# A hybrid decoder layer on one core: 80 small weight columns stored as 128, and another order of steps

## The chip, the cores and the metric

The kernel runs on one core of one Trainium2 chip. The time is the device time of one execution in microseconds. A run is one execution; the kernel before has three of them, and one more execution was taken with the profiler on. TensorE (PE in the views) multiplies, VectorE (DVE), ScalarE (ACT) and GpSimd (POOL) do the rest, and SyncE (SP) issues the transfers. Each engine works through its own queue in order.

## What is computed

One layer: an adaptive RMSNorm of x, one projection into all the small parts, two head groups side by side, and an output projection with a gated, normalised residual. Group A is a gated delta rule with chunks; group B picks 256 keys for each query with an indexer and attends to latents.

```python
mod = silu(c) @ w_ada + b_ada
shift, scale, gate = split(mod, 3)
h = rmsnorm(x, g_pre) * (1 + scale) + shift
qkv_a, z_a, b_a, a_a, q_b, ckv, z_b, iq, ik, iw = split(h @ w_in)
o_a = gated_deltanet(qkv_a, z_a, b_a, a_a, ...)     # conv, l2norm, triangular inverse per chunk, recurrence
o_b = dsa_sparse_attention(q_b, ckv, iq, ik, iw, ...)  # indexer score, top 256, softmax, w_uv
x = x + gate * rmsnorm(concat(o_a, o_b) @ w_out, g_post)
```

There are 1024 tokens and 1024 model columns; group A has 4 heads of 128 with chunks of 64, group B 4 heads of 128 and 8 indexer heads of 64. All is float32; large products are split into a high and a low part and done as three matmuls.

## The kernel before

The work is cut into named steps, and the table `PLAN` (lines 37 to 42) gives the order in which they are written down. A step is the next piece of a Python generator: `D0` and `D1` are the two token halves of the indexer keys, `F` the first token half of four convolutions, `X` the second token half of h, `I` the indexer scores (12 pieces), `S` the bitwise search for the 256th score (20), `K`, `J`, `Q`, `V`, `M`, `R`, `N`, `A` with a 0 or 1 the keys, the inverse, the queries, the values, the merge of the inverse's blocks, the recurrence, the norm and the mixing of a pair of group A's heads, `Z` its gates, `HZ` and `HQ` the gates and queries of group B, `C` the latents, `G` the residual gate, `T` an attention block and `O` an output block. A scheduler then interleaves what the steps issue within each engine's queue. A second table, `ENGINES`, names for 281 places (a split, an add, a copy) the engine that does it, where it is not the usual one.

Weights come as 25 tiles of 128 columns, fetched in the order in which the steps of `PLAN` need them, one raw tile ahead and two split ones. `split` (236 to 239, by the helpers at 174 to 181) makes a high part by a cast and a low part by a difference. `proj` (lines 421 to 433) does a half of 512 tokens: for each of the eight chunks of 128 model columns one matmul of the high weights with the high part of h (line 430), one with its low part (431), one of the low weights (432), into one of two PSUM banks. Whoever reads the bank last sets it free for the half after the next one.

The places that matter here:

- `wsp` (lines 391 to 398) holds 80 columns: 64 of the indexer key, 8 of its weights, 8 of group A's decay and write gates. `key_half` (440 to 450) runs `proj` on it, 24 matmuls for each token half, and copies the parts out. The host puts the 80 columns together in `laid_out`.
- `first_halves` (749 to 768) runs one-column products (line 754) for the first halves of four convolutions.
- `second_half` (452 to 466) transposes x on TensorE (line 311), makes h's high part on ACT (459), a float32 copy on VectorE (460) and the low part on POOL or VectorE (site `xl`).
- `conv_half` (704 to 731) scales the projection's bank and adds three shifted copies, on VectorE (line 189) or on ACT and POOL (192, 193).
- `invert` (858 to 878) is a chain of 60 POOL instructions, then two transfers through DRAM; `merge` (914 to 946) begins with a VectorE transpose of what came back (919) and goes on with small matmuls (926 to 942) and VectorE copies (927, 939). `recur` (948 to 1000) is a chain of 128-column matmuls, VectorE and ACT.
- `search` counts on VectorE (607) and ACT (619), and ends with six blocks of a comparison, a scan and two more passes (691 to 696).

## Time and profile before

| | us |
|---|---|
| median of 3 runs | 738.63 |
| the runs | 738.37, 738.63, 744.95 |
| the profiled execution | 746.19 |
| its span, first to last instruction | 744.5 |
| TensorE busy in it | 685.7 |
| VectorE busy | 529.7 |
| ACT busy | 436.9 |
| POOL busy | 336.3 |

The profiled execution is 7.6 us above the median, and 1.7 us of it lie outside the span. The granted clock is a share of 2.4 GHz; 0.50 is 1.2 GHz, the lower of the two levels that the rows show. A matmul's duration contains a part that overlaps the next one: in a dense row 512 columns start 0.23 us apart at the full clock and 0.43 at half.

### The profile page before, as it was taken

The page shows a single profiled execution, that of the slowest core. Times are in us where ns is not written, and L with a number is a line of the kernel's source. Part 1 is how long each engine was busy: PE and PEld are TensorE (multiplying, and loading weights), DVE is VectorE, ACT ScalarE, POOL GpSimd, SP SyncE. Part 2 cuts the span into 40 slices and gives each one's busy share as a digit, 9 for nine tenths or more (in the row PEclk, how much of TensorE's full clock was granted, in tenths as well). Part 3 has the DMA queues.
Part 4 walks back from the last instruction along what each step waited for, and adds up shares of the span by engine and source line. Part 5 has one row for each costly group of instructions (what it writes and reads, how often), then busy time and mean ns, then how long its engine had stood idle before and what let it go on. Part 6 is the DMA issues. An engine that isn't in the chain of part 4 may idle for free.

```text
span 744.5 us, 11292 instructions
## 1 busy us (share of the span) xinstructions
PE 685.7 (92%) x3863; PEld 574.7 (77%) x3863; DVE 529.7 (71%) x1342; ACT 436.9 (59%) x863; POOL 336.3 (45%) x395
## 2 busy tenths in 40 slices
PE   3999898999999899998998999988887999999996
PEld 2887787888778678876787878777765889888885
DVE  3977785663356866868689887877889999964212
ACT  4545584576668888859868494523336687434211
POOL 2146616456997300314432599941243232654310
PEclk9996999999999999999999999996799999999999
DMA  8931000013112111220032212276033205313311
GB/s 309 405 153 44 1 29 28 1 40 104 42 47 96 43 68 47 90 81 29 1 114 113 86 57 86 71 250 235 15 115 114 85 29 185 114 61 124 141 58 56
DMA packets 35287, 70.10 MB, mean 94 GB/s; under 512 B 11431, under 2 KB 18717, under 8 KB 35230
## 3 DMA queue, kind: packets, MB, share of 16 engines
q1 hardware_dynamic: 35230, 69.39, 26.5%
q8 instruction: 30, 0.49, 0.3%
q14 instruction: 27, 0.22, 0.1%
HBM read 53.64 MB, written 15.73 MB: 93 GB/s over the span
## 4 chain that ended last, share of the span: by engine, by line
PE 54%; DVE 16%; POOL 11%; DMA 6%; ACT 6%; issue 5%; SPq 1%; DVEq 0%; POOLq 0%; ACTq 0%
PE ps L430 8%; PE ps L432 8%; PE ps L431 8%; PE ps L1281 4%; PE ps L1279 4%; PE ps L1280 4%; POOL ns L869 4%; POOL rk L867 4%; ACT junk L619 2%; DVE pr L1217 1%; PE ps L1234 1%; DMA wraw<-in_w_tiles_dram 1%; DMA wa<-in_w_ada_dram 1%; DVE junk L607 1%; PE ps L579 1%
## 5 line engine op out<-in xcount | busy, mean ns | idle before, releaser
L430 PE MATMUL ps<-h,whi 128*128 128x512 f32 (+2 forms) x448 | 177.2, 396 | 12.8 <-DVE cv L189 6.7
L431 PE MATMUL ps<-h,whi 128*128 128x512 f32 (+2 forms) x448 | 177.0, 395 | 0.0
L432 PE MATMUL ps<-h,wlo 128*128 128x512 f32 (+2 forms) x448 | 176.0, 393 | 0.7 <-POOL wlo L181 0.7
L619 ACT ACTIVATE junk<-score,pat,sgn 128x1024 bf16<-128x1024 f32 (+2 forms) x93 | 105.5, 1135 | 11.5 <-DVE pat L660 10.3
L430 PEld LDWEIGHTS ps<-h,whi 128*128 128x128 f32 (+1 forms) x448 | 85.5, 191 | 34.2 <-DVE cv L189 7.8
L432 PEld LDWEIGHTS ps<-h,wlo 128*128 128x128 f32 (+1 forms) x448 | 85.4, 191 | 17.3 <-issue 0.9
L431 PEld LDWEIGHTS ps<-h,whi 128*128 128x128 f32 (+1 forms) x448 | 85.4, 191 | 15.9 <-issue 0.7
L607 DVE TENSOR_SCALAR_CACHE_REDUCE junk<-score,pat 128x640 bf16<-128x640 f32 (+2 forms) x93 | 68.8, 740 | 1.6
L193 POOL TENSOR_TENSOR cv<-cv,tmp 128x510 f32<-128x510 f32 (+2 forms) x33 | 39.1, 1186 | 42.6 <-ACT tmp L192 42.3
L1281 PE MATMUL ps<-woh,ml 128*128 128x512 f32 x128 | 49.9, 392 | 1.3 <-DVE ml L181 1.3
L590 ACT ACTIVATE ps<-ps 128x512 f32<-128x512 f32 (+3 forms) x70 | 34.1, 511 | 28.5 <-PE ps L580 27.9
L1280 PE MATMUL ps<-wol,mh 128*128 128x512 f32 x128 | 50.4, 394 | 0.0
L1279 PE MATMUL ps<-woh,mh 128*128 128x512 f32 x128 | 50.0, 393 | 0.0
L193 POOL TENSOR_TENSOR score<-score,tmp 128x512 f32<-128x512 f32 (+3 forms) x29 | 32.4, 1123 | 35.0 <-ACT tmp L192 30.7
L189 DVE SCALAR_TENSOR_TENSOR score<-ps,iw,score 128x384 f32<-128x384 f32 (+3 forms) x41 | 25.7, 643 | 28.1 <-ACT ps L590 22.8
L869 POOL TENSOR_TENSOR ns<-ns,rk 64x30 f32<-64x30 f32 (+14 forms) x60 | 36.1, 602 | 3.8
L181 POOL TENSOR_TENSOR wlo<-wraw,whi 128x1024 fp32r<-128x1024 f32 (+1 forms) x11 | 25.7, 2340 | 26.7 <-PE ps L432 19.9
L867 POOL TENSOR_TENSOR rk<-ns 64x30 f32<-64x30 f32 (+14 forms) x60 | 36.2, 604 | 3.2
L189 DVE SCALAR_TENSOR_TENSOR cv<-ps,cols,cv 128x511 f32<-128x511 f32 (+2 forms) x39 | 28.8, 738 | 6.2 <-POOL cv L193 4.3
L174 ACT ACTIVATE whi<-wraw 128x1024 fp32r<-128x1024 f32 x19 | 20.0, 1054 | 20.1 <-PE ps L431 12.7
L1283 ACT ACTIVATE junk<-ps 128x512 bf16<-128x512 f32 x16 | 9.5, 595 | 36.8 <-PE ps L1281 32.3
L181 DVE TENSOR_TENSOR wlo<-wraw,whi 128x1024 fp32r<-128x1024 f32 x19 | 24.7, 1299 | 8.7 <-ACT whi L174 7.8
(358 smaller groups left out, 1742.1 us busy)
## 6 DMA issues: line engine op xcount, KB each, us to landing
wraw<-in_w_tiles_dram SPq DMA_DIRECT2D x29, 512.0 KB, 3.5
wa<-in_ada_tiles_dram SPq DMA_DIRECT2D x16, 512.0 KB, 10.2
x<-in_x_dram SPq DMA_DIRECT2D x8, 512.0 KB, 3.3
qd<-qo SPq DMA_DIRECT2D x8, 512.0 KB, 3.0
wa<-in_w_ada_dram SPq DMA_DIRECT2D x8, 512.0 KB, 5.1
qb<-qd SPq DMA_DIRECT2D x8, 512.0 KB, 3.2
woraw<-in_w_out_dram SPq DMA_DIRECT2D x8, 512.0 KB, 3.4
xr<-in_x_dram SPq DMA_DIRECT2D x8, 512.0 KB, 3.9
```

The source lines that it names most:

```text
L189: V.scalar_tensor_tensor(o, a, scale, o, op0=ALU.mult, op1=ALU.add)
L193: G.tensor_tensor(o, o, tmp, op=ALU.add)
L430: mm(o, lhsT=hi[:, k, :], rhs=h[:, 0, c0:c1], start=(k == 0), stop=False)
L431: mm(o, lhsT=hi[:, k, :], rhs=h[:, 1, c0:c1], start=False, stop=False)
L432: mm(o, lhsT=lo[:, k, :], rhs=h[:, 0, c0:c1], start=False, stop=(k == NK - 1))
L607: V.tensor_scalar(junk[:, 0:src.shape[1]], src, t, None, op0=op, op1=ALU.add, accum_out=o)
L619: A.activation(junk[:, 0:(b + 1) * P], score[b], AF.Sign, scale=sg, bias=t, accum_out=o)
L867: G.tensor_tensor(tmp, ns[:, 0:i, i:i + 1].to_broadcast([64, i, w]), ns[:, i:i + 1, i + 1:32].to_broadcast([64, i, w]), op=ALU.mult)
L869: G.tensor_tensor(ns[:, 0:i, i + 1:32], ns[:, 0:i, i + 1:32], tmp, op=ALU.add)
L1279: mm(ps, lhsT=mh[:, k, :], rhs=woh[k][:, sl], start=(k == 0), stop=False)
L1280: mm(ps, lhsT=mh[:, k, :], rhs=wol[k][:, sl], start=False, stop=False)
L1281: mm(ps, lhsT=ml[:, k, :], rhs=woh[k][:, sl], start=False, stop=(k == NK - 1))
```

## The change

The tile of 80 columns gets 48 more, from the indexer's queries, so that weights, matmuls and PSUM rows are 128 wide. Only the first 80 rows are copied out. `PLAN` is another order of the same steps, and 86 places of `ENGINES` name another engine.

```diff
-PLAN = ("D0 F F X X X D1 F I F E I I K0 K0 I I I K0 I I K0 I I I I K0 HZ J0 J0 J0 J0 J0 J0 J0 J0 J0 J0 J0 J0 J0 "
+PLAN = ("F F X D0 X X D1 F I F E I I I K0 K0 I I I K0 I K0 I I I I K0 J0 J0 S S S S J0 S J0 J0 J0 Q0 HZ HZ J0 "
...
-    wsp_raw = blk((P, NK, 80), name="wraw")
+    wsp_raw = blk((P, NK, P), name="wraw")
...
-    wsp = split("wsp", wsp_raw, *(w[:, :, 0:80] for w in wsp_parts))
+    wsp = split("wsp", wsp_raw, *wsp_parts)
...
-        copy(f"sp{hf}", sp[0:80, sl], ps)
+        copy(f"sp{hf}", sp[0:80, sl], ps[0:80, :])
...
-    small = np.concatenate([w_in[:, OFF_IK:OFF_IK + 72], w_in[:, OFF_BA:OFF_BA + 8]], axis=1)
+    small = np.concatenate([w_in[:, OFF_IK:OFF_IK + 72], w_in[:, OFF_BA:OFF_BA + 8], w_in[:, OFF_IQ:OFF_IQ + 48]], axis=1)
...
-    return {"in_w_tiles_dram": tiles, "in_w_small_dram": columns(small, 0, 80), "in_ada_tiles_dram": np.array(ada)}
+    return {"in_w_tiles_dram": tiles, "in_w_small_dram": columns(small, 0, P), "in_ada_tiles_dram": np.array(ada)}
```

The 25 weight tiles come in the same order but for one exchange: the first value tile now stands before the first gate tile of group A (before: Z0 V0 V0 Z0, now V0 Z0 V0 Z0). Of the places in `ENGINES`, by count ten score adds, three convolution adds and five casts of weights go from ACT and POOL to VectorE; six copies of values, one input scaling (`xn0`, to POOL), one difference of h (`xl7`, to POOL) and some adds of three columns change as well. VectorE has 20 instructions more (1260 for 1240), ACT 25 fewer and POOL 5 fewer.

TensorE's queue at the first key half (`ps` is the bank, `whi` and `wlo` the small weights, `h` a chunk of h, L754 a one-column product), before:

```order
L341 MATMUL ps_473<-ones,acc_456 128x1 x4
L430 MATMUL ps_579<-h_489,whi_497 80x512
L431 MATMUL ps_579<-h_489,whi_497 80x512
L754 MATMUL ps_609<-shc_103,wraw_132 128x1 x2
L754 MATMUL ps_638<-shc_103,wraw_150 128x1 x2
L432 MATMUL ps_579<-h_489,wlo_498 80x512
L430 MATMUL ps_579<-h_490,whi_497 80x512
L431 MATMUL ps_579<-h_490,whi_497 80x512
```

And in the changed kernel:

```order
L341 MATMUL ps_473<-ones,acc_456 128x1 x4
L754 MATMUL ps_579<-shc_103,wraw_132 128x1 x2
L754 MATMUL ps_608<-shc_103,wraw_150 128x1 x2
L430 MATMUL ps_653<-h_489,whi_497 128x512
L431 MATMUL ps_653<-h_489,whi_497 128x512
L432 MATMUL ps_653<-h_489,wlo_498 128x512
L430 MATMUL ps_653<-h_490,whi_497 128x512
L431 MATMUL ps_653<-h_490,whi_497 128x512
```

The one-column products now stand ahead of the half's first matmul, and its output has 128 rows. Further on, of eight transposes of x (L311) that stood inside this half four are left; the others follow it.

VectorE's queue at the first value tiles (`cv` is the first tile's convolution, L189 one of its adds, L919 the transposes with which the first pair's merge begins, L607 a count of the search), before:

```order
L919 STREAM_TRANSPOSE T_2707<-X_1446 128x1024
L181 TENSOR_TENSOR wlo_2461<-wraw_2334,whi_2460 128x1024
L607 TENSOR_SCALAR junk_2230,cnt_2127<-score_816,pat_2129 128x512
L919 STREAM_TRANSPOSE T_2870<-X_1769 128x1024
L920 MEMSET T_2707 32x8x32
L607 TENSOR_SCALAR junk_2232,cnt_2127<-score_815,pat_2129 128x384
L178 TENSOR_SCALAR vn_2408<-ps_2409,gv_560 128x128
L920 MEMSET T_2870 32x8x32
L189 SCALAR_TENSOR_TENSOR cv_2329<-ps_2373,cols,cv_2329 128x509
L728 TENSOR_TENSOR cv_2329<-cv_2329,last_2327 128x3
```

And in the changed kernel:

```order
L919 STREAM_TRANSPOSE T_2657<-X_1440 128x1024
L607 TENSOR_SCALAR junk_1882,cnt_1809<-score_816,pat_1811 128x512
L181 TENSOR_TENSOR wlo_2365<-wraw_2273,whi_2364 128x1024
L919 STREAM_TRANSPOSE T_2820<-X_1751 128x1024
L920 MEMSET T_2657 32x8x32
L607 TENSOR_SCALAR junk_1884,cnt_1809<-score_815,pat_1811 128x384
L178 TENSOR_SCALAR vn_2345<-ps_2346,gv_560 128x128 x2
L189 SCALAR_TENSOR_TENSOR cv_2268<-ps_2310,cols,cv_2268 128x509
L920 MEMSET T_2820 32x8x32
```

In both the tile's last add (`128x509`) stands behind the two transposes; the weights split there (`wlo`) are those of the tile after the next one, and which tile uses the PSUM bank next is now a gate's, not a value's.

VectorE's queue at the merge of the second pair (L927 and L939 are the merge's copies, L691 to L696 the blocks at the search's end, L1059 a weighted sum of the residual gate), before, from the first L927 on:

```order
L927 COPY qsb_4624<-ps_4622 32x8x32
L694 SCALAR_TENSOR_TENSOR keep_4929<-cum_4927,cnt_2127 128x1
L695 SCALAR_TENSOR_TENSOR eq_4928<-cum_4927,keep_4929,eq_4928 128x768
L696 SCALAR_TENSOR_TENSOR score_814<-score_814,pat_2129,eq_4928 128x768
L178 TENSOR_SCALAR mask_4911<-score_814 128x768
L691 TENSOR_SCALAR eq_4939<-score_815,pat_2129 128x640
L693 SCALAR_TENSOR_TENSOR cum_4938<-eq_4939 128x640
L694 SCALAR_TENSOR_TENSOR keep_4940<-cum_4938,cnt_2127 128x1
L695 SCALAR_TENSOR_TENSOR eq_4939<-cum_4938,keep_4940,eq_4939 128x640
L927 COPY qsb_4624<-ps_4622 32x8x32
L696 SCALAR_TENSOR_TENSOR score_815<-score_815,pat_2129,eq_4939 128x640
L1059 SCALAR_TENSOR_TENSOR gac_4969<-wa_4979,cs,gac_4969 128x1024
```

And in the changed kernel, from the first L927 on:

```order
L927 COPY qsb_4660<-ps_4658 32x8x32
L1059 SCALAR_TENSOR_TENSOR gac_5059<-wa_5072,cs,gac_5059 128x1024
L694 SCALAR_TENSOR_TENSOR keep_4916<-cum_4914,cnt_1809 128x1
L695 SCALAR_TENSOR_TENSOR eq_4915<-cum_4914,keep_4916,eq_4915 128x640
L696 SCALAR_TENSOR_TENSOR score_815<-score_815,pat_1811,eq_4915 128x640
L927 COPY qsb_4660<-ps_4658 32x8x32
L939 COPY qsb_4660<-ps_4707 64x512
L693 SCALAR_TENSOR_TENSOR cum_4925<-eq_4926 128x512
L1059 SCALAR_TENSOR_TENSOR gac_5059<-wa_5075,cs,gac_5059 128x1024
```

Before the merge's first copy the changed queue has already done the 768-wide block and the 640-wide scan; between the first two copies four rows stand in place of eight.

## Rows read from the trace of the kernel before

**Rows 1.** The page, busy us of each engine, share of the span, instructions.

```profile
PE 685.7 (92%) x3863; PEld 574.7 (77%) x3863; DVE 529.7 (71%) x1342; ACT 436.9 (59%) x863; POOL 336.3 (45%) x395
```

**Rows 2.** Stretches: length, busy us (instructions) by engine, PEclk, DMA share, GB/s.

```profile
core 0: us, PE busy (x) PEld busy (x) DVE busy (x) ACT busy (x) POOL busy (x), PEclk, DMA share, GB/s
...
58.50:72.50 14.00, 13.28 (x47) 10.08 (x47) 10.67 (x20) 7.27 (x13) 8.09 (x8) 0.51 0.17 55
72.50:93.00 20.50, 18.56 (x111) 14.73 (x110) 15.68 (x25) 10.06 (x16) 13.57 (x17) 1.00 0.01 2
...
157.00:327.00 170.00, 164.02 (x927) 134.51 (x925) 104.89 (x277) 128.77 (x235) 86.01 (x119) 0.98 0.19 65
...
357.00:507.00 150.00, 142.05 (x754) 117.47 (x755) 121.40 (x274) 88.85 (x175) 88.87 (x111) 1.00 0.32 108
507.00:530.00 23.00, 18.98 (x185) 16.96 (x183) 17.15 (x28) 7.79 (x20) 3.57 (x2) 0.55 0.37 127
530.00:562.00 32.00, 28.07 (x166) 21.91 (x165) 26.87 (x75) 14.67 (x51) 12.73 (x11) 0.95 0.28 94
```

**Rows 3.** Two of the short stretches with a lower granted clock.

```profile
123.50:127.50 4.00, 4.00 (x12) 3.13 (x11) 2.15 (x4) 1.50 (x3) 1.50 (x2) 0.57 0.00 0
...
253.00:257.00 4.00, 4.00 (x11) 3.16 (x12) 3.11 (x10) 3.91 (x8) 0.27 (x2) 0.57 0.00 0
```

**Rows 4.** Order of time, TensorE: start, length, instruction, idle before and releaser.

```profile
59.62 0.72 PE L432 MATMUL ps<-h,wlo 128*80 128x512 f32 x1 [0.72 <-POOL wlo L181]
...
63.98 3.41 PE L754 MATMUL ps<-shc,wraw 128*128 128x1 f32 x16
...
69.02 1.91 PE L311 MATMUL ps<-ident,x 128*128 128x128 f32 x8
```

**Rows 5.** Groups by line and shape: count, busy us, mean ns of one, idle before.

```profile
L430 PEld LDWEIGHTS ps<-h,whi 128*128 128x128 f32 x432 | 82.5, 191 | 32.6 <-DVE cv L189 7.8 <-ACT tmp L192 3.5 <-ACT zo L1029 3.1
L430 PEld LDWEIGHTS ps<-h,whi 128*80 128x80 f32 x16 | 3.0, 189 | 1.5 <-issue 0.7 <-ACT tmp L192 0.2
...
L189 DVE SCALAR_TENSOR_TENSOR score<-ps,iw,score 128x512 f32<-128x512 f32 x11 | 8.2, 746 | 10.3 <-ACT ps L590 9.6 <-POOL score L193 0.5 <-POOL dt L540 0.2
L176 DVE CAST whi<-wraw 128x1024 fp32r<-128x1024 f32 x10 | 8.2, 815 | 0.0
L189 DVE SCALAR_TENSOR_TENSOR score<-ps,iw,score 128x320 f32<-128x320 f32 x10 | 5.3, 546 | 3.9 <-ACT ps L590 3.9
...
L181 POOL TENSOR_TENSOR wlo<-wraw,whi 128x1024 fp32r<-128x1024 f32 x10 | 23.9, 2387 | 26.7 <-PE ps L432 19.9 <-ACT whi L174 6.0 <-PE ps L754 0.7
L193 POOL TENSOR_TENSOR cv<-cv,tmp 128x510 f32<-128x510 f32 x13 | 15.0, 1154 | 26.5 <-ACT tmp L192 26.4
L181 POOL TENSOR_TENSOR wlo<-wraw,whi 128x640 fp32r<-128x640 f32 x1 | 1.9, 1867 | 0.0
```

**Rows 6.** Order of time, POOL, low parts of h in both token halves.

```profile
65.33 1.43 POOL L406 TENSOR_TENSOR h<-xhT,h 128x512 fp32r<-128x512 f32 x1
...
82.55 3.79 POOL L181 TENSOR_TENSOR h<-hf,h 128x512 fp32r<-128x512 f32 x3
```

**Rows 7.** Order of time, TensorE, at the first value tiles.

```profile
252.96 0.51 PE L430 MATMUL ps<-h,whi 128*128 128x512 f32 x1 [2.88 <-DVE cv L189]
...
267.79 0.47 PE L430 MATMUL ps<-h,whi 128*128 128x512 f32 x1 [1.07 <-DVE ok L659]
```

**Rows 8.** Order of time, VectorE, before the first of these waits ends.

```profile
249.89 1.23 DVE L919 STREAM_TRANSPOSE T<-X 128x1024 f32<-128x1024 f32 x1
...
252.29 0.61 DVE L189 SCALAR_TENSOR_TENSOR cv<-ps,cols,cv 128x509 f32<-128x509 f32 x1
```

**Rows 9.** Order of time, VectorE, the second pair's inverse comes back.

```profile
486.69 1.25 DVE L919 STREAM_TRANSPOSE T<-X 128x1024 f32<-128x1024 f32 x1 [4.91 <-DMA X<-scr]
```

**Rows 10.** Order of time, VectorE, inside the second pair's merge.

```profile
499.74 0.16 DVE L694 SCALAR_TENSOR_TENSOR keep<-cum,cnt 128x1 f32<-128x1 f32 x1
...
503.10 1.49 DVE L693 TENSOR_TENSOR_SCAN cum<-eq 128x640 f32<-128x640 bf16 x1
...
513.19 1.28 DVE L1059 SCALAR_TENSOR_TENSOR gac<-wa,cs,gac 128x1024 f32<-128x1024 f32 x1
```

More of the change, by code (lines that the diff above doesn't have):

```diff
@@ L35 @@
 NWS = NRAW + 4
-PLAN = ("D0 F F X X X D1 F I F E I I K0 K0 I I I K0 I I K0 I I I I K0 HZ J0 J0 J0 J0 J0 J0 J0 J0 J0 J0 J0 J0 J0 "
[4 rows of a table removed]
-        "O2 O7 O7 O5 O2").split()
+PLAN = ("F F X D0 X X D1 F I F E I I I K0 K0 I I I K0 I K0 I I I I K0 J0 J0 S S S S J0 S J0 J0 J0 Q0 HZ HZ J0 "
[4 rows of a table added]
+        "O6 O5 O7 O2 O4 O5 O2").split()
 PARTS = {"HZ": (4, (0, 1, 2, 3)), "HQ": (4, (0, 1, 2, 3)), "I": (12, (0, 3, 6, 9)), "S": (20, ()), "G": (2, ()), "B": (1, ()), "C": (2, (0,)), "W": (8, ()),
@@ L56 @@
 ADA = ((2, 2, 4), (1, 1, 2, 2, 2))
-ENGINES = {"ad00": "V", "ad01": "V", "ad20": "V", "ad30": "V", "ad50": "V", "cT0": "V", "cT1": "V", "cv011": "A",
[37 rows of a table removed]
+ENGINES = {"ad00": "V", "ad01": "V", "ad11": "V", "ad20": "V", "ad30": "V", "ad50": "V", "cT0": "V", "cT1": "V",
[37 rows of a table added]
 SITES = {}
```

82 rows, old and new, of tables (ENGINES, PLAN) are left out of this document.

## The prediction

> **What bounds the kernel now.** I read the page's busy shares first, then a table of stretches, then the order of time on TensorE and on the engines that it waits for. TensorE is the engine to follow: it is busy for 685.7 us of the span, VectorE for 529.7 [rows 1]. A busy TensorE is not yet a fast one, so the second view is the granted clock by stretch. From 58.5 to 72.5 TensorE is busy for 13.28 of 14 us, but the granted clock is 0.51, that is nearly all of it at 1.2 instead of 2.4 GHz; between 507 and 530 it is 0.55 [rows 2]. The other dips are shorter: each of two windows of 4 us shows 0.57, which is (1 - 0.57) x 4 = 1.7 us lost and 2 x 1.7 = 3.4 us at 1.2 GHz [rows 3]. The long dip at 58.5 holds 0.49 x 14 = 6.9 us of loss, four times as much. Its rows say what runs there: the last products of one column (L754), a wait for the low part of the small weights, and then the 24 matmuls of the first key half, on 80 columns of weights, among 16 more passes of L754 that take 3.41 us and transposes [rows 4]. Before it fell, TensorE ran one-column products and then had a gap of 0.72 us; it came back inside the 80-column matmuls, by 72.5 [rows 2].
>
> **The change part by part.** The sum is made against the profiled execution, 746.2 us (span 744.5), and carried over to the median of 738.6, which is 7.6 us lower. That the runs lie that far apart without any edit is a caution: some of the losses counted below may be smaller in the other runs.
>
> *Filled columns.* 48 matmuls keep their 512 columns of output stream, so their count and length at one clock do not change. The load of 80 columns takes 189 ns and that of 128 takes 191 ns [rows 5]: 48 x 2 ns = 0.1 us. The Trainium skill (TensorE: Matmul & The Clock Gate, section LDWEIGHTS (loading the stationary operand)) says that a load's time grows with its columns, which speaks against the change: an estimate by its formula is 40 ns for each of 48 loads, 1.9 us. This case's rows do not show that growth, and the sum goes by the rows. The DMA grows from 320 to 512 KB while VectorE is still in a chain of seven weighted sums; it is hidden. The cast of the high part on VectorE leads nowhere, as POOL takes the low part up after its own queue. There 1.87 us become 2.39 [rows 5]; TensorE waits for just this, so 0.5 us is lost before the first L432.
>
> *The clock in the first key half.* No row of before shows 128-column matmuls right after this fall. Bounds: nothing comes back (0), or the whole dip goes (6.9). The nearest rows are the dips in 128-column matmuls, 3.4 us at 1.2 GHz [rows 3]. If this dip is as short, 14 x 0.49 x 2 = 13.7 us at half clock become 3.4, and the same work takes 10.3 / 2 = 5.1 us less. Less the 0.5 above that is 4.6. But what follows does not wait for TensorE alone. The matmul of the sixth chunk needs POOL's difference (L406, 65.33 + 1.43 = 66.8 us), and that hangs on VectorE and ACT, not on TensorE [rows 6]. The transposes behind it then run at about 66.5 instead of 69.0, and with them starts POOL's chain of differences for the second token half: seven, the last three ending at 82.55 + 3.79 = 86.3 [rows 6], and an eighth on VectorE, which is POOL's too now and costs the chain some 1.3 us more. Between 72.5 and 93 TensorE is busy for 18.6 of 20.5 us and POOL for 13.6 [rows 2], so part of what is gained is waited for again: by the chain 2 to 3 us are left, by TensorE 4.6. I take 4, nearer to TensorE, which is the busier of the two; ends -0.5 and 6.4. The order supports it: two groups of L754 now stand ahead of the first key matmul, and four of eight transposes move behind the half's end, so less low-clock work is spread through it.
>
> *Values and gates, 243 to 275.* Before, two value projections, whose results need three more adds each, stand next to each other on the weight list (Z0 V0 V0 Z0); now they alternate with gates (V0 Z0 V0 Z0), which need one ACT instruction per half. TensorE waited there 2.88 us for a convolution's add and 1.07 us for VectorE once more [rows 7], and a dip of 1.7 us lies behind it [rows 3]: 5.6 us. The add stood behind two transposes of 1.2 us, a weight difference and counts on VectorE [rows 8]. It still does, as the order shows, so the first wait is not gone by order alone: the gate's second half needs the same PSUM bank. What eases is the pile behind it. Ends: 5.6, or as much again lost if the transposes are later than the add. I take 2.5, a little under half.
>
> *Inverse, merge and recurrence of the second pair.* POOL has two convolution adds fewer among the 60 instructions of the second inverse, about 2.3 us at 1.15 each [rows 5]; VectorE stood 4.91 us at the merge's first transpose, waiting for that inverse [rows 9]. Two steps of the search come ahead of the latents. Counted from the merge's first copy (L927) to the first softmax row (L1217), VectorE has one 640-element scan, the end of one 768-element block and one weighted sum less: 1.49 + 0.16 + 1.02 + 1.02 + 0.56 + 0.55 + 1.28 = 6.1 us (the first and the last of the block's six rows, and the weighted sum, stand in [rows 10]). Over 507 to 562 VectorE is busy for 17.2 + 26.9 = 44 of 55 us [rows 2]. But the first 23 us are small matmuls at 1.2 GHz with TensorE busy 19.0, and an easier VectorE does not speed those. Ends 0 and 6.1; I take 2.5, nearer to the 11 us that VectorE is idle than to the 44.
>
> *What moves onto VectorE.* Ten score adds (0.55 to 0.75 us), three convolution adds and five casts (0.82) leave ACT and POOL for it, 5.9 + 2.2 + 4.1 = 12 us (the widest and the narrowest score add and the cast stand in [rows 5]). All come before 507. Cover: VectorE is idle for 65 us between 157 and 327 and for 29 between 357 and 507 [rows 2]. Ends 0 and 12 lost; I take 1, by the waits of 1 to 3 us that a full VectorE queue costs now [rows 7]. The first scaling of an input tile moves to POOL, which waits for the next tile's sums then: nothing. More output matmuls stand at the very end and fewer among the attention steps; TensorE works without a gap in both places, so this shifts work and adds none.
>
> Sum: 4 + 2.5 + 2.5 - 1 = 8.0 us. 746.2 becomes 738.2 in an execution like the profiled one; 738.6 becomes **730.6**.
>
> **The rivals.**
> *The clock stays low.* The key half runs at 1.2 GHz as before, its 0.5 us of wait added. For it: TensorE had no gap from 59.62 on and the clock still did not rise until 72.5 [rows 2, 4]. Against it: the dips with 128 columns were short [rows 3]. Price: the 4 go, the rest stays: 734.6. The Trainium skill (same page, section What's actually happening) says that the throttle is released by activity; if that were all, the fill would bring nothing, as TensorE was active already. The trace does not agree with it here.
> *Given back in the middle.* The new order makes two new waits of 2.3 us, each with a dip of 1.7 us, in place of those it removes: 730.6 + 8 = 738.6, no change. For it: the wait of 2.88 us had such a dip behind it [rows 3, 7].
> *VectorE becomes the bound (slower).* Place: 157 to 327 and 357 to 507, where search counts, convolution adds and casts share one queue and PSUM banks are freed by its adds. The 12 us are then paid in full, and the value stretch and the merge gain nothing: 738.6 - 4 + 12 = 746.6. It decides from the point at which TensorE's waits for VectorE in these two stretches together grow by over 10 us. Against it: the idle time above.
> *All of it comes.* 6.4 + 5.6 + 6.1 - 1 = 17; with half of the last doubtful, 723.
>
> **How the numbers follow.** Forecast 0.44, clock low 0.16, given back 0.14, slower 0.13, all of it 0.13. A measurement of this kernel tells about 1% (7.4 us) from no change. Of the forecast's 0.44, whose own range is 725 to 735, 0.31 lies below 731.2 and 0.13 above; with 0.13 of the full gain and 0.02 of the low-clock case, faster is 0.46; same is 0.13 + 0.14 + 0.14 = 0.41; slower 0.13. The range leaves out the last of the full gain and half of the slower case: 720 to 742.
>
> **What would show it.** Right: in the first key half the matmuls stand 0.23 us apart again by about 63, and the second half ends near 88 instead of 92; the wait before it grows to some 1.2 us; TensorE's wait at the value projections is under 2 us; VectorE's wait for the merged inverse shrinks. Wrong: a granted clock near 0.5 still at 70 us (the first rival), new waits of over 2 us for VectorE between 93 and 507 (the second and third), or a merge and recurrence as long as the 55 us of before, which would make the last 2.5 us a count without effect.

## The result and the profile after

| | before | changed |
|---|---|---|
| median of 20 runs each, us | 741.37 | 736.67 |
| ratio to before | | 0.9947, 95% interval 0.9925 to 0.997 |
| the profiled execution, us | 746.19 | 737.11 |
| its span, us | 744.5 | 735.3 |

The changed kernel is half a per cent faster; 1.1% was forecast. The two profiles lie 9.1 us apart, the medians 4.7: the first profile of before was one of its longer executions, and this turned out to be a part of the answer. One of the 20 runs before took 3652.32 us; the ratio leaves it out, and without it the median before is 739.86 and the medians lie 3.2 us apart. A second profile of the unchanged kernel, taken later (739.75 us, span 738.0), is used below beside the first.

The page's busy times of the changed kernel (as [rows 1]): VectorE has 20 instructions more, TensorE 5 us less.

```profile
PE 680.8 (93%) x3863; PEld 572.9 (78%) x3863; DVE 533.5 (73%) x1362; ACT 425.3 (58%) x838; POOL 333.1 (45%) x390
```

Stretches of the changed kernel, columns as in [rows 2]:

```profile
57.00:72.00 15.00, 12.64 (x58) 9.80 (x58) 13.63 (x23) 8.78 (x15) 10.82 (x12) 0.77 0.14 45
72.00:92.00 20.00, 18.30 (x99) 15.43 (x100) 13.43 (x21) 8.89 (x14) 13.63 (x14) 0.91 0.02 7
243.00:275.00 32.00, 31.11 (x177) 24.73 (x176) 26.85 (x76) 28.33 (x55) 5.85 (x9) 1.00 0.26 99
460.00:472.00 12.00, 9.47 (x36) 7.39 (x35) 11.49 (x14) 4.54 (x10) 10.98 (x16) 0.86 0.44 142
498.00:521.50 23.50, 18.93 (x193) 16.97 (x189) 15.08 (x25) 7.28 (x20) 1.57 (x1) 0.56 0.43 150
521.50:554.50 33.00, 28.75 (x178) 22.45 (x177) 27.81 (x84) 15.65 (x52) 11.80 (x9) 1.00 0.34 112
```

Read against [rows 2 and 3]: at the first key half the clock is 0.77 where it was 0.51. In the next 20 us it now falls too (0.91, that is 0.09 x 20 = 1.8 us lost), where before it held 1.00. The value tiles run at 1.00 with TensorE busy 31.1 of 32 us. Between 460 and 472 TensorE is idle for 2.5 us and the clock falls: new. The merge at 498 is as before, 0.56 for 0.55.

TensorE in both key halves of the changed kernel, in order of time (start, length, instruction, idle before and releaser):

```profile
59.58 0.79 PE L432 MATMUL ps<-h,wlo 128*128 128x512 f32 x1 [0.99 <-POOL wlo L181]
60.17 0.63 PE L430 MATMUL ps<-h,whi 128*128 128x512 f32 x1
60.60 0.63 PE L431 MATMUL ps<-h,whi 128*128 128x512 f32 x1
...
66.05 0.40 PE L431 MATMUL ps<-h,whi 128*128 128x512 f32 x1
66.28 0.40 PE L432 MATMUL ps<-h,wlo 128*128 128x512 f32 x1
...
70.63 0.66 PE L311 MATMUL ps<-ident,x 128*128 128x128 f32 x4 [0.75 <-DVE hf L460]
71.91 0.47 PE L430 MATMUL ps<-h,whi 128*128 128x512 f32 x1 [0.63 <-DVE sp L176]
74.08 0.98 PE L311 MATMUL ps<-ident,x 128*128 128x128 f32 x4 [1.70 <-DVE hf L460]
```

The starts are 0.43 us apart at 60 and 0.23 at 66: the clock came back about where the forecast had it, by 64 (the second profile of before, further down, does so too, without the fill). But the gap ahead of the first L432 is 0.99 us ([rows 4] had 0.72), and within the second half TensorE stands three times, 3.1 us together, each time for VectorE. VectorE's queue at that place shows why:

```profile
69.77 0.80 DVE L460 TENSOR_SCALAR hf<-ps,sc,shc 128x512 f32<-128x512 f32 x1
70.49 0.67 DVE L176 CAST khi<-ps 64x512 fp32r<-64x512 f32 x1
71.09 0.67 DVE L176 COPY sp<-ps 80x512 f32<-80x512 f32 x1
71.79 1.39 DVE L449 CAST khi<-khi 64x512 fp32r<-64x512 f32 x1
73.22 0.81 DVE L460 TENSOR_SCALAR hf<-ps,sc,shc 128x512 f32<-128x512 f32 x1
```

The second float32 copy of h (`hf`, L460), which frees the bank for the next transposes, stands behind three copies of the finished key half and starts at 73.22; the transposes follow at 74.08, and a stretch of low clock behind them.

Further on, the waits of [rows 7] and the new one:

```profile
252.31 0.50 PE L430 MATMUL ps<-h,whi 128*128 128x512 f32 x1 [0.76 <-ACT tmp L192]
...
463.51 0.80 PE L430 MATMUL ps<-h,whi 128*128 128x512 f32 x1 [2.53 <-DVE qo L1144]
464.11 0.63 PE L431 MATMUL ps<-h,whi 128*128 128x512 f32 x1
```

2.88 us at the value tiles became 0.76. The wait of 2.53 us at 463.5 is new, with low clock behind it (0.63 us a matmul). VectorE ahead of it:

```profile
454.98 2.48 DVE L693 TENSOR_TENSOR_SCAN cum<-eq 128x1024 f32<-128x1024 bf16 x1
...
457.85 1.58 DVE L695 SCALAR_TENSOR_TENSOR eq<-cum,keep,eq 128x1024 bf16<-128x1024 f32 x1
...
459.95 1.49 DVE L181 TENSOR_TENSOR wlo<-wraw,whi 128x1024 fp32r<-128x1024 f32 x1
461.37 1.48 DVE L696 SCALAR_TENSOR_TENSOR score<-score,pat,eq 128x1024 f32<-128x1024 f32 x1
462.78 0.68 DVE L1144 SCALAR_TENSOR_TENSOR qo<-ps,qo 128x512 fp32r<-128x512 f32 x1
...
477.38 1.24 DVE L919 STREAM_TRANSPOSE T<-X 128x1024 f32<-128x1024 f32 x1
```

The search's first end block (scan, L695, L696) and a weight split now lie ahead of the difference (L1144) that frees the bank of the last query product; in both profiles of before that scan started 2.5 us after the difference had ended. In the second profile of the changed kernel the wait is there too (2.66 us), but the low clock lies behind the next wait, one of 3.01 us at 476.4. The last row answers to [rows 9]: the merge's transpose starts with no idle time ahead, so VectorE's 4.91 us are gone.

How far the work had come, in us, by the last instruction of each stage in the order of time:

| | first key half | second key half and first tile | 28th of 56 projection groups of 24 matmuls | last projection | recurrence | last output matmul |
|---|---|---|---|---|---|---|
| before, first profile | 73.5 | 92.2 | 281.1 | 506.1 | 562.7 | 737.6 |
| before, second profile | 69.0 | 88.0 | 272.8 | 499.4 | 555.9 | 731.1 |
| changed | 69.2 | 91.4 | 271.1 | 497.4 | 554.2 | 728.4 |
| changed without the fill | 69.0 | 88.2 | 267.8 | 493.7 | 547.9 | 721.3 |

Against the second profile the change wins nothing in the first key half, loses 3.4 us by the end of the second, and wins 5.1 from there to the middle. About half of the 5.1 has no term in the prediction's sum: from the end of the second key half to the end of the twelfth projection group the second profile of before takes 68.1 us and the changed kernel 65.6, for the same work to within one or two matmuls. In both profiles of before TensorE waits there 1.8 us in the indexer's products, with low clock behind it; in the changed kernel this wait is gone. The second profile of before:

```profile
117.84 0.58 PE L579 MATMUL ps<-khi,qe 128*128 128x512 f32 x1 [1.80 <-DVE qe L565]
```

### The profile page after: what moved, and what is told of

Same layout as the page of the kernel before. It is cut to its first block, busy times and chain, and to the rows that moved or that the text cites. A ratio compares the mean times of both kernels' runs of the same rounds, so it can differ in the third digit from the quotient of the medians.

```text
span 735.3 us, 11298 instructions
## 1 busy us (share of the span) xinstructions
PE 680.8 (93%) x3863; PEld 572.9 (78%) x3863; DVE 533.5 (73%) x1362; ACT 425.3 (58%) x838; POOL 333.1 (45%) x390
## 4 chain that ended last, share of the span: by engine, by line
PE 55%; DVE 14%; POOL 12%; ACT 8%; DMA 5%; issue 5%; SPq 1%; DVEq 0%; POOLq 0%; ACTq 0%
PE ps L430 7%; PE ps L431 7%; PE ps L432 7%; POOL ns L869 4%; POOL rk L867 4%; PE ps L1280 4%; PE ps L1279 4%; PE ps L1281 4%; ACT junk L619 2%; PE ps L1234 2%; PE ps L580 1%; PE ps L579 1%; DVE junk L607 1%; POOL cv L193 1%; PE ps L1241 1%
## 5 line engine op out<-in xcount | busy, mean ns | idle before, releaser
L430 PE MATMUL ps<-h,whi 128*128 128x512 f32 (+1 forms) x448 | 176.8, 395 | 10.8 <-ACT tmp L192 3.0
L432 PE MATMUL ps<-h,wlo 128*128 128x512 f32 (+1 forms) x448 | 174.5, 390 | 1.0 <-POOL wlo L181 1.0
L431 PE MATMUL ps<-h,whi 128*128 128x512 f32 (+1 forms) x448 | 175.4, 392 | 0.0
L430 PEld LDWEIGHTS ps<-h,whi 128*128 128x128 f32 x448 | 85.5, 191 | 30.6 <-ACT tmp L192 5.8
L432 PEld LDWEIGHTS ps<-h,wlo 128*128 128x128 f32 x448 | 85.4, 191 | 17.5 <-POOL wlo L181 1.7
L431 PEld LDWEIGHTS ps<-h,whi 128*128 128x128 f32 x448 | 85.6, 191 | 14.9
L607 DVE TENSOR_SCALAR_CACHE_REDUCE junk<-score,pat 128x640 bf16<-128x640 f32 (+2 forms) x93 | 68.7, 739 | 2.5 <-ACT score L174 1.2
L189 DVE SCALAR_TENSOR_TENSOR score<-ps,iw,score 128x384 f32<-128x384 f32 (+3 forms) x50 | 31.8, 645 | 31.3 <-ACT ps L590 26.9
L193 POOL TENSOR_TENSOR cv<-cv,tmp 128x509 f32<-128x509 f32 (+2 forms) x30 | 35.7, 1189 | 36.6 <-ACT tmp L192 36.3
L181 POOL TENSOR_TENSOR wlo<-wraw,whi 128x1024 fp32r<-128x1024 f32 x10 | 24.3, 2427 | 30.2 <-issue 10.2
L193 POOL TENSOR_TENSOR score<-score,tmp 128x512 f32<-128x512 f32 (+3 forms) x20 | 22.7, 1136 | 32.6 <-ACT tmp L192 24.8
L189 DVE SCALAR_TENSOR_TENSOR cv<-ps,cols,cv 128x511 f32<-128x511 f32 (+2 forms) x42 | 31.2, 744 | 5.7 <-POOL cv L193 3.7
L181 POOL TENSOR_TENSOR wol<-woraw,woh 128x1024 fp32r<-128x1024 f32 x8 | 20.3, 2560 | 25.4 <-ACT woh L174 24.7
L534 POOL TENSOR_TENSOR gm<-triU,gdp 128x512 fp32r<-128x512 f32 x16 | 16.5, 1045 | 30.8 <-PE ps L537 22.4
```

What stands on the lines that cost most here:

```text
L189: V.scalar_tensor_tensor(o, a, scale, o, op0=ALU.mult, op1=ALU.add)
L193: G.tensor_tensor(o, o, tmp, op=ALU.add)
L430: mm(o, lhsT=hi[:, k, :], rhs=h[:, 0, c0:c1], start=(k == 0), stop=False)
L431: mm(o, lhsT=hi[:, k, :], rhs=h[:, 1, c0:c1], start=False, stop=False)
L432: mm(o, lhsT=lo[:, k, :], rhs=h[:, 0, c0:c1], start=False, stop=(k == NK - 1))
L607: V.tensor_scalar(junk[:, 0:src.shape[1]], src, t, None, op0=op, op1=ALU.add, accum_out=o)
```

## The experiments

Sixteen runs. "Without the fill" means 80 columns again. The column on the clock is (1 - granted clock) x 20 us from the window 54 to 74 us of each profile, the loss at the first key half. The runs were made in four groups, each on one chip beside runs of before, whose medians there are 739.85, 739.69, 739.94 and 740.5 us; the ratio is against those runs and is not the quotient of the two medians.

| run | median, us | ratio to before, 95% interval | loss at 54 to 74 |
|---|---|---|---|
| fill_alone | 740.26 | 1.0004, 0.9978 to 1.0029 | 3.4 |
| plan_alone | 742.55 | 1.0019, 0.9996 to 1.0043 | 1.8 |
| engines_alone | 749.38 | 1.01, 1.006 to 1.014 | 3.4 |
| change_without_fill | 730.03 | 0.9865, 0.983 to 0.9901 | 1.8 |
| changed_again | 736.96 | 0.996, 0.9931 to 0.999 | 3.4 |
| split128_mm80 | 737.33 | 0.9954, 0.9927 to 0.998 | 3.4 |
| small_split_act_dve | 733.07 | 0.9915, 0.9879 to 0.995 | 3.4 |
| before_again | 739.75 (1 run) | | 3.4 |
| eq7_on_pool | 738.11 | 0.9963, 0.9934 to 0.9991 | 1.8 |
| small_split_80 | 732.06 | 0.9864, 0.9825 to 0.9903 | 1.8 |
| value_first_order | 732.79 | 0.9883, 0.9845 to 0.9921 | 1.8 |
| moves_back | 742.23 | 1.003, 0.9998 to 1.0062 | 1.8 |
| scores_back | 738.22 | 0.9967, 0.9942 to 0.9991 | 3.4 |
| convs_back | 738.9 | 0.9968, 0.9937 to 1.0 | 6.8 |
| splits_back | 744.97 | 1.0064, 1.0037 to 1.009 | 3.4 |
| only_23_moves | 741.45 | 1.0031, 1.0003 to 1.0058 | 1.8 |

### The three parts of the change by themselves

The fill put into the kernel before; `PLAN` alone; `ENGINES` alone; and the changed kernel with the fill taken out, which is

```diff
-    wsp_raw = blk((P, NK, P), name="wraw")
+    wsp_raw = blk((P, NK, 80), name="wraw")
-    wsp = split("wsp", wsp_raw, *wsp_parts)
+    wsp = split("wsp", wsp_raw, *(w[:, :, 0:80] for w in wsp_parts))
```

with the copy and the host's columns to match.

> The kernel before with the 48 filled columns only; order of steps and engines as before. Theory A (the fill shortens the low-clock stretch, and the second key half gives most of it back): at the first key half the 1.2 GHz stretch falls from 13.7 us to about 7, the half ends 3 to 4 us earlier, but TensorE then waits 2 to 3 us more inside the second half for VectorE's float32 copies of h and POOL's differences; the time is 0 to 2 us lower (ratio 0.997 to 1.000). Theory B (the clock gain arrives in full): 4 us lower, ratio 0.9945, no new wait in the second half. Theory C (the dip went because of the new order, not because of the columns): the clock is still about 0.5 from 60 to 72, the time is 0 to 1 us higher.

> The kernel before with the new order of steps only; 80 columns, engines as before. Theory A (the gain of the change sits in the order of steps, at the value and gate tiles): TensorE's wait of 2.9 us for a convolution's add at the value tiles is under 1 us, a new wait near 460 for VectorE's search blocks costs 2 to 4; in all 1 to 4 us lower (0.995 to 0.999). Theory B (the gain is the fill's): within 1 us of before, and a long stretch at half clock at the first key half. Theory C (all from the order): 5 us lower and the first key half at the full clock by about 65.

> The kernel before with the 86 changed places of the engine table only. Theory A (the places are worth little by themselves): within 2 us of before, VectorE busy some 4 us longer, ACT some 10 us less. Theory B (the moves relieve ACT and POOL where TensorE waits for them): 3 to 5 us lower. Theory C (the places fit only the new order): 3 us or more higher, with new waits of TensorE for VectorE between 157 and 507.

> The changed kernel with 80 columns again: order and engines as changed. Theory A (the fill brings 0 to 2 us here too): 735 to 739, 3 to 5 us lower than before, with a long stretch at half clock at the first key half that the wait in the second half then partly hides. Theory B (the fill's gain arrives in full): within 1 us of before, 741. Theory C (the fill does nothing): as the changed kernel, 0.5% lower than before, and a 1.2 GHz stretch at the first key half as short as the changed kernel's 6.8 us.

None of the three theories foresaw the last: without the fill the kernel is at 0.9865, some 7 us below the changed one. The fill is no gain that is hidden, it is a loss. In the old order it moves nothing that the interval shows, but the place is the same: fill_alone ends the second key half at 91.4, the second profile of before at 88.0, and the stretch at half clock in the first half is as short in both (6.8 us), so the short stretch that theory A expected of the fill is not the fill's. And neither table gains alone: the order is 0.2% slower (its interval reaches no change), the engines 1%, both together 1.35% faster.

The order by itself fits none of its theories: TensorE's wait at the value tiles is still 2.22 us, now for ACT, and no new wait stands near 460. That one comes with the engines, whose run fits its theory C: beside a wait of 5.30 us for VectorE at 241 it has

```profile
465.88 0.79 PE L430 MATMUL ps<-h,whi 128*128 128x512 f32 x1 [2.44 <-DVE qo L1144]
```

TensorE and VectorE of the version without the fill, at the rows shown of the changed kernel:

```profile
58.48 0.71 PE L432 MATMUL ps<-h,wlo 128*80 128x512 f32 x1 [0.16 <-POOL wlo L181]
...
60.67 0.39 PE L431 MATMUL ps<-h,whi 128*80 128x512 f32 x1
60.90 0.39 PE L432 MATMUL ps<-h,wlo 128*80 128x512 f32 x1
...
69.86 0.66 PE L311 MATMUL ps<-ident,x 128*128 128x128 f32 x4 [0.20 <-DVE hf L460]
...
72.67 0.66 PE L311 MATMUL ps<-ident,x 128*128 128x128 f32 x4 [0.44 <-DVE hf L460]
...
75.95 0.65 PE L311 MATMUL ps<-ident,x 128*128 128x128 f32 x4 [1.20 <-DVE hf L460]
```

```profile
68.14 0.81 DVE L460 TENSOR_SCALAR hf<-ps,sc,shc 128x512 f32<-128x512 f32 x1 [0.32 <-ACT h L459]
...
68.99 0.81 DVE L460 TENSOR_SCALAR hf<-ps,sc,shc 128x512 f32<-128x512 f32 x1
69.71 0.67 DVE L176 CAST khi<-ps 64x512 fp32r<-64x512 f32 x1
```

With 80 columns the matmuls stand 0.23 us apart already at 60.7, so 80 columns do not hold the clock down. And two copies of h stand ahead of the key's copies, where the changed kernel has one: there the scheduler, given a longer split, had put four transposes, and with them their copy, behind.

### Which part of the fill costs

The changed kernel again; the same with 128 columns fetched and split but 80 in the matmuls; and with 128 everywhere, but the split on ACT and VectorE:

```diff
-    wsp = split("wsp", wsp_raw, *wsp_parts)
+    wsp = tuple(w[:, :, 0:80] for w in split("wsp", wsp_raw, *wsp_parts))
...
-"wsph": "V"
+"wsph": "A", "wspl": "V"
```

> The changed kernel as it is, beside the next two on one chip. Theory A (what the fill costs sits in the two key halves: VectorE's first two float32 copies of h fall behind the copies of the key, TensorE waits 3.1 us and a 1.2 GHz stretch of 3.4 us follows; POOL's longer low part adds a gap of 1 us in the first half): 735 to 737, 0.4 to 0.8% lower than before, some 6 us above the version without the fill. Theory C (the two were timed on different chips and do not differ): 730 to 732, as the version without the fill.

> The changed kernel with 128 columns fetched and split, but only 80 of them given to the 48 matmuls: the order on VectorE and ACT is the changed kernel's. Theory A (order and split): 735 to 737 as the changed kernel, with the same wait of about 3 us in the second key half. Theory B (the 128 columns in the matmuls cost): 730, as without the fill. My first idea, that 80 columns hold the clock low, would make it slower than the changed kernel by 3 us or more, with a stretch of over 10 us at 1.2 GHz in the first key half.

> The changed kernel, 128 columns everywhere, but the high part of the small weights is made on ACT and the low part on VectorE (1.2 us there for POOL's 2.7), which also puts VectorE's second and third float32 copies of h ahead again. Theory A: TensorE's gap before the first low-weight matmul is under 0.3 us, the waits of 0.75, 0.63 and 1.70 us in the second half fall to 1.5 us together, no 1.2 GHz stretch at 74; 729 to 732, 0.6 to 0.9% below the changed kernel. Theory B (the columns cost): as the changed kernel, 735 to 737.

Theory A holds in the first two: 736.96 and 737.33, so the matmuls' width is worth nothing that these runs show, and the cost sits in the longer split and the order that comes of it. The loads of the weights do depend on the width. From 75 to 93 us of the first profile of before, at a clock of 1.00, by groups as in [rows 5]:

```profile
L430 PEld LDWEIGHTS ps<-h,whi 128*128 128x128 f32 x8 | 1.5, 188 | 0.4
...
L430 PEld LDWEIGHTS ps<-h,whi 128*80 128x80 f32 x6 | 0.9, 147 | 0.5
```

Between 60 and 72, at half the clock, a load of 80 columns takes 251 ns; the mean of 189 in [rows 5] is one over both levels. Matmuls of either width start 0.23 us apart all the same, so the 40 ns do not reach the time.

In the third the matmuls are 128 wide, the low part comes early and the copies of h are ahead:

```profile
57.88 0.63 PE L432 MATMUL ps<-h,wlo 128*128 128x512 f32 x1
...
70.83 0.65 PE L311 MATMUL ps<-ident,x 128*128 128x128 f32 x4 [0.40 <-DVE hf L460]
...
74.09 0.66 PE L311 MATMUL ps<-ident,x 128*128 128x128 f32 x4 [1.17 <-DVE hf L460]
```

The gap is gone, the waits are 1.6 us for 3.1, the second half ends at 86.5 for 91.4, and 4 of the 7 us come back (733.07, a little short of theory A's 729 to 732). The last projection ends at 491.1, 6 us earlier than the changed kernel's and earlier than without the fill (493.7). Against the version without the fill 5.9 us are lost again behind it; 3.4 of them are low clock (20.5 us at half clock in the merge for 17.1, 6.8 after the recurrence for 3.4), and the rest is not traced. So the place is shown; that these two edits are the whole cost is not.

> The kernel before once more, for a second profile of it. Theory A (its executions differ by where TensorE's clock falls): the stretch at 1.2 GHz at the first key half is shorter than the 13.7 us of the first profile in an execution near 738, and the sum of all such stretches is lower by about twice the difference in time; the work and the waits are the same. Rival (the executions differ by transfers or waits): the low stretches are the same and TensorE's idle time is longer by the difference.

This is the run that undid the first term. The same kernel, the same queue, by the granted clock (ninth figure) of the window 54 to 74:

```profile
54.00:74.00 20.00, 19.35 (x102) 14.63 (x103) 17.49 (x29) 13.37 (x21) 15.82 (x16) 0.83 0.13 41
```

0.17 x 20 = 3.4 us are lost here, half of the 6.9 of [rows 2]. At this place theory A of its text holds: the first key half ends at 69.0 for 73.5, with the same instructions. For the whole it holds in part: by the mean granted clocks of the two spans (0.964 of 744.5 us, 0.969 of 738.0) they lost 26.8 and 22.9 us, which is 3.9 of the 6.5 us between them. Waits differ as well: the first one at the value tiles is 1.70 us here, without low clock behind it.

> The changed kernel without the fill, and the split of the 80 small columns on ACT and VectorE as in the run with 128. Theory A (the gap before the first low-weight matmul is only 0.16 us here, so there is little to win): within 1.5 us of the version without the fill, 728.5 to 731. Rival (the early split is worth in itself the 4 us that it brought with 128 columns): 726. If 128 columns cost nothing in the matmuls and the order is as good, this and the run with 128 columns and this split should agree within 2 us.

The early split with 80 columns: 732.06, ratio 0.9864, not to be told from 0.9865. Where no gap is left there is nothing to win. Against the run with this split and 128 columns (733.07, 0.9915) the medians agree within the 2 us of its text, the ratios less well and with intervals that overlap: whether the wider tile still costs something there is open.

### The value tiles and the new wait

The old order of the first value and gate tiles, and the end block's first comparison on POOL, both without the fill:

```diff
-J0 V0 Z0 J0 V0 Z0 S J0
+J0 Z0 V0 J0 V0 Z0 S J0
...
+"eq7": "G"
```

> The changed kernel without the fill, with the old order of the first value and gate tiles (gate, value, value, gate). Theory A (as predicted, the alternation of values and gates is worth about 2.5 us): the wait for a convolution's add comes back at the second value tile with 1.5 to 3 us; 732 to 734, ratio 0.989 to 0.992. Rival (the wait went because the merge's two transposes no longer stand ahead of that add at that time, not for the order of the tiles): within 1 us of the version without the fill, 0.9865.

2.8 us slower in the median, 0.7 against small_split_80, which ran beside it, 1.3 by the two ratios: the intervals overlap, and the whole time does not settle it. The profile does at this stage: 3.5 us are lost by the last projection before the first recurrence (316.5 for 313.0; 313.2 in small_split_80), 1.7 of them in low clock behind the second wait, and both waits are for a convolution's add again. Theory A, for the place:

```profile
243.54 0.50 PE L430 MATMUL ps<-h,whi 128*128 128x512 f32 x1 [1.93 <-DVE cv L189]
...
257.47 0.50 PE L430 MATMUL ps<-h,whi 128*128 128x512 f32 x1 [1.83 <-DVE cv L189]
```

> The changed kernel without the fill, and the comparison of the search's first end block (1024 columns) on POOL in place of VectorE; by its order this puts the last query product's scaling and difference ahead of that block's scan on VectorE. Theory A (the wait of 2.5 us near 460, new in the changed kernel, is VectorE's search block ahead of that difference, and the 1.2 GHz stretch of 3.4 us behind it belongs to it): the wait is under 0.8 us, the stretch is gone, 2 to 4 us less than without this edit: 726 to 728, ratio 0.981 to 0.985. Rival (POOL's 2.9 us for the comparison delay the inverse that it is in, and the merge waits for that): the wait at 460 goes but the recurrence starts no earlier; 729 to 731, ratio 0.986.

It is 8 us slower than without the edit, worse than the rival said. The wait at 463.5 is halved, and ten us later a longer one takes its place. TensorE, POOL and ACT:

```profile
464.13 0.50 PE L430 MATMUL ps<-h,whi 128*128 128x512 f32 x1 [1.18 <-ACT tmp L192]
...
474.34 1.12 PE L778 MATMUL ps<-ident,cv 128*128 128x128 f32 x4 [4.47 <-ACT cv L731]
```

```profile
450.39 3.73 POOL L691 TENSOR_SCALAR eq<-score,pat 128x1024 bf16<-128x1024 f32 x1
...
472.55 1.08 POOL L193 TENSOR_TENSOR cv<-cv,tmp 128x509 f32<-128x509 f32 x1
```

```profile
473.65 0.63 ACT L731 ACTIVATE cv<-cv 128x512 f32<-128x512 f32 x1 [9.00 <-POOL cv L193]
```

POOL takes 3.73 us for a comparison that cost VectorE about 1.1, and a convolution's adds, behind the inverse in POOL's queue, come that much later; ACT stands 9 us for them, then TensorE for ACT. That the block stands ahead of the difference is read from the queue; a version without the wait was not reached.

### The moves onto VectorE

Nine places of score adds, five of convolution adds and nine of weight splits on the engines of before (23 of 86), then each kind by itself, then the 23 alone with the other 63 put back; all without the fill.

> The changed kernel without the fill, with 23 places (the score adds, the convolution adds, the weight splits) on the engines of before again; the other 63 stay. Theory A (these moves onto VectorE are what makes the new order pay: ACT and POOL were late there): 4 us or more slower than the version without the fill, 734 or above, and TensorE's new waits are for ACT or POOL between 90 and 320. Theory B (as predicted: the moves cost VectorE about 1 us and bring nothing): 1 us faster to 1 us slower, 729 to 731. Theory C (the other places matter, those of the recurrence and the attention steps): under 2 us, with the difference behind 500.

Put back (shown by the first of each kind):

```diff
+"s161": "A", "cv1011": "A",
-"w1152h": "V", "w1152l": "V",
...
```

Theory A is right in size: 742.23 for 730.03, 12 us. The longest waits are for convolutions:

```profile
424.82 0.63 PE L430 MATMUL ps<-h,whi 128*128 128x512 f32 x1 [3.70 <-DVE cv L189]
...
472.10 0.50 PE L430 MATMUL ps<-h,whi 128*128 128x512 f32 x1 [2.67 <-ACT tmp L192]
...
482.36 0.66 PE L778 MATMUL ps<-ident,cv 128*128 128x128 f32 x4 [2.93 <-ACT cv L731]
```

but at 320 only 2.3 us are lost; most goes behind 415, not between 90 and 320 as its text said.

> The changed kernel without the fill, the nine places of score adds on ACT and POOL again. Theory A (the score adds free POOL and ACT in the indexer stage, 93 to 150, so that the next steps start earlier): 3 us or more slower than without the fill, 733 or above, lost before 320. Theory B (the convolution adds carry the 12 us): within 1.5 us of 730.

> The changed kernel without the fill, the five places of convolution adds as before. Theory B (a convolution on ACT and POOL queues behind the 60 instructions of the inverse and behind counts, and the PSUM bank it reads is freed late): 4 us or more slower, 734 or above, with waits of TensorE of over 2 us between 415 and 490. Theory A: within 1.5 us of 730.

> The changed kernel without the fill, the nine places of weight splits as before. Theory C (casts of 0.8 us on VectorE for 1.1 on ACT, low parts of 1.2 us for POOL's 2.4, keep the weights ahead): 2 us or more slower, 732 or above. Rival (weights are split a whole tile ahead, so it is hidden): within 1.5 us of 730.

> The changed kernel without the fill, with the 23 places of score adds, convolution adds and splits of the change, the other 63 as before. If the 23 carry the gain: 729 to 733, within 3 us of the version with all 86. If the 63 (values, recurrence, attention) are needed as well: 735 or above, lost behind 500.

Each kind alone costs 8 to 15 us; their sum, 32, is far above the 12 of all three at once, and the 23 without the 63 give nothing either. No kind carries the gain: it belongs to the whole table. The sizes are above the 2 to 4 us that the texts ask for, and the 63 are needed as well, though what is missing without them is lost ahead of 500 (the last projection ends at 501.3 for 493.7), not behind it. What the four have in common is the place: new or longer waits stand where TensorE needs a PSUM bank, in one or more of the stretches 230 to 255, near 420 and 460 to 485. The costliest run's waits of TensorE for whom (us in total, times, longest), between 90 and 510:

```profile
PE ps L430 <- ACT tmp L192: 9.7, 4, 5.4
PE ps L430 <- ACT zo L1029: 4.1, 4, 2.3
PE ps L430 <- DVE pat L660: 2.7, 1, 2.7
```

The profile of convs_back also shows the long stretch at the first key half again:

```profile
54.00:74.00 20.00, 19.39 (x91) 15.19 (x91) 14.90 (x27) 10.28 (x17) 14.09 (x15) 0.66 0.12 41
```

0.34 x 20 = 6.8 us lost. Its queues, and those of value_first_order and eq7_on_pool, are the same on all engines as without the fill until well behind both key halves; the version without the fill and those two lost 1.8.

## Why the prediction was wrong, and where it was right

**Filled columns (about 0, 0.5 lost).** Right for the matmuls: 128 and 80 columns give 736.96 and 737.33. The reading of the loads was wrong: 189 and 191 ns are means over different clocks, and at the full clock a load grows from 147 to 188 ns, close to the estimate of 40 that the prediction set aside; it is hidden, so the sum is not touched. The 0.5 us for POOL's longer low part was 0.8 (0.99 less 0.16), 1.2 in the second profile of the changed kernel. Missed was what the longer split does to the order.

**The clock in the first key half (4 won).** This is the step that failed, twice. First, "the long dip at 58.5" was taken as the kernel's; it was that execution's: kernels with the same queues lost 1.8 or 6.8 us there. Fourteen profiles with 80 columns in the matmuls lost 1.8 us (seven), 3.4 (five) or 6.8 (two), 3.1 on average; the four with 128 lost 3.4 each. The sign that the prediction named for being right, starts 0.23 us apart by about 63, came with the fill and, in the second profile of before, without it: that it came was luck. The fill gives no clock back on average; that it keeps the longest case away cannot be told from four. The clock rises in 80-column matmuls, at 60.7 in one profile, by 72.5 in another. The Trainium skill (TensorE: Matmul & The Clock Gate, section What's actually happening) says that activity releases the throttle and that the moment varies between runs of one kernel. The runs agree with it, and the prediction set it aside on the evidence of one profile. Second, "The order supports it: ... four of eight transposes move behind the half's end, so less low-clock work is spread through it" read the loss as a gain. Those transposes took their copies of h behind the key's on VectorE: 3.1 us of waits (1.8 without the fill) and 1.8 of clock in the second half, where 0.6 was allowed for (4 taken of 4.6). In place of 4 won, the fill costs about 7 in the medians (736.96 less 730.03). Of these, 3.2 stand in the profiles by the end of the second half (91.4 for 88.2); nearly all the rest comes behind the last projection (see below).

**Values and gates (2.5 won).** Right in the mechanism, and in size as far as it can be told: 3.5 in the profiles of the single edit at that stage, 0.7 to 2.8 in the medians, which the noise does not separate from nothing. As argued, the order alone does not take the first wait away (2.22 us in plan_alone); with both tables it is 0.76. The 5.6 us taken as the upper end held a dip of 1.7 and a wait of 2.88 that the second profile of before shows as no dip and 1.70.

**Inverse, merge and recurrence (2.5 won).** Nothing came in the changed kernel: from the last projection to the recurrence's end 562.7 - 506.1 = 56.6 us before (56.5 in its second profile), 554.2 - 497.4 = 56.8 after. VectorE did get free of its 4.91 us, but TensorE's clock from 498 is 0.56, as it was, and the merge goes no faster; the text's own sign of a count without effect, a merge and recurrence as long as before, is met. Without the fill the stretch took 54.2 us with 17.1 us at half clock in place of 20.5; whether a part of the 2.5 would come at an equal clock is open.

**Moves onto VectorE (1 lost).** The sign was wrong. With the new order they are worth about 12 us, with the old order all 86 places cost 1%. The step that failed is that the sum priced only what VectorE pays and put what ACT and POOL are spared at nothing. With moves taken back TensorE waits longer for banks: ahead of L430 and L778 between 90 and 510 us 9.5 us in all without the fill, 11.3 to 17.2 in the four runs. In the costliest of them 13.8 us are for ACT, but in moves_back the longest wait is for VectorE (3.70); why the whole table is needed is not shown.

**The rivals.** "Given back in the middle" came true at one place, as priced: 2.53 us of wait, and 1.7 of clock; but it is the engine table that brings this wait, not the new order. "VectorE becomes the bound" did not come in the changed kernel. "The clock stays low" had the right term (no gain from the fill) for a wrong reason.

So the half per cent (4 us by the ratio) is about 10 won by the two tables together and some 6 to 7 lost by the fill. In the profiles 3.4 of the fill's 7.1 us arise behind the last projection. What stays open is how much of that is the fill's, as profiles of one kernel differ there too: the changed kernel's two profiles have 20.5 and 17.1 us of low clock from 498 on in the merge, and 6.8 and 3.4 after the recurrence. The second has there as much as the version without the fill, and from the last projection to the last output matmul it takes 229.6 us for 227.6: 2.0 in place of 3.4.

## What to carry to other kernels

Take a second profile of the unchanged kernel before pricing a clock dip, a transfer or anything else that the code does not fix: the largest term here rested on one execution. When a tile grows, look at what its longer preparation does to the order of the queues around it, and follow every copy that frees a bank; an instruction that moves behind a boundary takes its readers along. Do not compare the mean lengths of two groups whose members ran at different clocks. The table that places work on engines could not be priced entry by entry here: each part of it that was taken out lost 8 us or more, so test the whole, and the one unrelated edit beside it (the fill) by itself; without it this change is, at 0.9865, as good as any version measured here.

## What was not expected of the hardware

The same queues on all engines ran the first key half at the lower of the two clock levels for 13.7 us in one execution and 6.8 in another (before), and for 13.7 and 3.4 in kernels that differ only later on (clocks of 0.66, 0.83 and 0.91 in 20 us). In the merge the stretch at half clock also differed between profiles of one kernel (20.5 and 17.1 us in the changed one). A weight load of 80 columns was shorter than one of 128 (147 and 188 ns at the full clock), and yet the matmuls of both started 0.23 us apart.
